# The first layer's modulation in smaller pieces, in front of the products that need it

## The chip, the cores and the metric

One core of one Trainium2 chip. The time is the device time of one execution in microseconds, given as the median of the runs.

## What is computed

A trunk of four layers over a sequence of 256 context rows and 256 rows of x, width 1024, in float32. The layers are a gated spatial unit (layer 0), an RWKV layer, an attention layer, and a gated spatial unit again (layer 3). Each layer first normalises its input and modulates it by a shift and a scale that come from a conditioning vector (one for the context, one for x). The case is about the start of layer 0:

```python
def ada_modulation(cond, w, b):
    m = jax.nn.silu(cond) @ w + b                       # w: 1024 x 3072
    shift, scale, gate = jnp.split(m, 3, axis=-1)
    return shift[..., None, :], scale[..., None, :], gate[..., None, :]

def sgu_mixer(h, w_in, gain, w_s, b_s, w_out):          # w_in: 1024 x 6144
    u, v, z = jnp.split(h @ w_in, 3, axis=-1)
    u = jax.nn.gelu(u)
    v = rms_norm(jax.nn.gelu(v), gain)
    ...
    return (s * jax.nn.silu(z)) @ w_out

# in reference(), layer i:
shift, scale, gate = ada_modulation(c, ada_w[i], ada_b[i])
h = rms_norm(x) * (1 + scale) + shift
x = x + gate * sgu_mixer(h, *sgu_args)                  # and the same for ctx with c_ctx
```

## The kernel before

The 512 rows (context and x) are held transposed as `xT`: eight blocks `k` of 128 features by 512 columns of time. Products are made in a split form: each float32 operand is cast to the narrower type `fp32r` as a high part, and the rest becomes a low part; hi·hi, hi·lo and lo·hi are summed, so that one product of blocks is three matmuls. A weight tile is loaded by `wload` (line 170): a transfer of 1 MB into `raw` (three buffers), a cast of the whole tile into `hi` on ScalarE (ACT, line 183) and a subtraction into `lo` on VectorE (DVE, line 184); `hi` and `lo` have two buffers each. `wparts` with `parts` over 1 does the cast and the subtraction in that many slices, of which all but the first have their subtraction on GpSimd.

**The modulation of layer 0.** Its weights (12 MB) are six chunks of 512 columns: chunks 0 and 1 are the shift, 2 and 3 the scale, 4 and 5 the gate, so that feature block k has its shift in chunk k // 4 and its scale in chunk 2 + k // 4. `ada_load` (line 201) brings a chunk in four transfers of 512 KB into tiles named `adaw`, taken from a ring of 20 buffers that also holds the pairs `hp`. `ada_first` (line 210) multiplies a chunk with the conditioning vectors: eight matmuls `adap` (two instructions each in the trace) in four column groups, a copy `m4` by ACT (line 221), four matmuls `adaT` with a selection matrix (eight instructions) that put the sums across the partitions and so turn them into columns, two additions of the bias on DVE (line 228, context and x), and for the scale one more for "1 +" (line 230). `m4`, the row norm `rstd` and the working tiles `h` share four buffers.

**The norm and the modulated blocks.** `norm_mod` (line 288) makes for each block k: `h = xT * rstd` on DVE (line 292), scale and shift of the context half on ACT (line 297) and of the x half on DVE (line 295), then the split, a cast on ACT (line 304) and a subtraction on DVE (line 305), into the pair `hp`.

**The value products.** In `sgu` (line 349) the columns of v are made in four blocks `c` of 512. For each there are two halves of the weights (`half`, four feature blocks each); each feature block k gives twelve matmuls (four row blocks of 128, three matmuls each, lines 375 to 377). So one half is 48 matmuls, and the whole of v is 384. In the text a "product" of these counts is one such matmul.

**The order around the change.** The program is written down in one sequence. A scheduler orders each engine's instructions when the program is built: of those that its model holds to be ready it takes the first in the written sequence, so that a later product can be put into a gap, and the order is then fixed. Transfers are issued on SyncE's queue (SP), in their order. Before, the sequence is: load chunk 0, the first value weights (transfer and cast), load chunk 2; the row norm; compute chunks 0 and 2, load chunks 1 and 3 (`first`); modulate blocks 0 to 3; the 48 products of half 0; compute chunks 1 and 3 (`early`), modulate blocks 4 to 7; load and cast the second value weights; the 48 products of half 1; then the other column blocks. Chunks 4 and 5 follow later in the layer (`later`). The other three layers' modulation is made on DVE (`ada_rest`, line 232), written behind the layer and put into gaps of it.

## Time and profile before

| | |
|---|---|
| median of 3 runs | 1621.2 us (1619.01 to 1622.14) |
| the profiled execution, its own time | 1616.74 us |
| its span, first to last instruction | 1615.0 us |
| TensorE busy | 1516.5 us (94%) |
| VectorE busy | 1151.3 us (71%) |
| ScalarE busy | 788.0 us (49%) |
| mean granted clock of TensorE | 0.97 |

The profile is of one execution. PE is TensorE's matmuls and PEld its weight loads, DVE is VectorE, ACT ScalarE, POOL GpSimd, SP SyncE. Matmuls are pipelined: a row's duration is longer than the step from one matmul to the next, which is read from their starts. The granted clock is a share of TensorE's full 2.4 GHz; 0.5 is its lower level, 1.2 GHz.

### The profile page before, as it was taken

What the parts mean: (1) busy time and instruction counts of PE and PEld (TensorE: products, weight loads), DVE (VectorE), ACT (ScalarE), POOL (GpSimd) and SP (SyncE); (2) the same over time, 40 slices, a digit from 0 to 9 for tenths busy, and PEclk for the clock granted to TensorE, in tenths of its full rate; (3) what the DMA queues carried; (4) which work ended last, traced back from release to release, by engine and by line L of the source; (5) the groups of instructions that cost most, each with busy time, mean ns of one, the idle gap of its engine ahead of it and who ended that gap; (6) DMA issues with size and microseconds to landing.
All of it is one profiled execution on the core that took longest, in us unless ns stands there. A gap on an engine that the chain in (4) does not pass through costs nothing.

```text
span 1615.0 us, 28890 instructions
## 1 busy us (share of the span) xinstructions
PE 1516.5 (94%) x11666; PEld 1173.8 (73%) x11666; DVE 1151.3 (71%) x2101; ACT 788.0 (49%) x1404; POOL 124.8 (8%) x156
## 2 busy tenths in 40 slices
PE   5999999999599998899899899899999999979998
PEld 2787888888467644777676677678777777768887
DVE  3789998845788367586796854778766666665876
ACT  4544231222455353444445333569866766456543
POOL 0000000000500142212303000000000000000000
PEclk8999999999799999799999999999999999989999
DMA  9676658631044553432433133134321232265452
GB/s 366 242 288 232 234 192 305 233 105 52 36 145 167 174 159 77 145 90 80 126 103 87 59 113 103 62 129 137 121 76 47 78 92 92 66 234 196 169 183 79
DMA packets 95174, 229.05 MB, mean 142 GB/s; under 512 B 26048, under 2 KB 52160, under 8 KB 80576
## 3 DMA queue, kind: packets, MB, share of 16 engines
q1 hardware_dynamic: 92736, 223.00, 41.1%
q10 hardware_dynamic: 2304, 4.20, 0.7%
q8 instruction: 92, 1.51, 0.4%
q14 instruction: 42, 0.34, 0.1%
HBM read 208.81 MB, written 17.83 MB: 140 GB/s over the span
## 4 chain that ended last, share of the span: by engine, by line
PE 46%; DVE 6%; ACT 6%; issue 1%; POOL 1%; DMA 0%; ACTq 0%; DVEq 0%; POOLq 0%
PE fm L310 4%; PE op L310 4%; PE pg L904 3%; PE op L975 2%; PE fm L311 2%; PE op L311 2%; PE pz L310 2%; PE pu L310 2%; PE po L1286 2%; PE sc L1304 2%; PE pe L790 2%; PE sc L1305 1%; PE pv L376 1%; PE pz L311 1%; PE pv L377 1%
## 5 line engine op out<-in xcount | busy, mean ns | idle before, releaser
L184 DVE TENSOR_TENSOR lo<-raw,hi 128x2048 fp32r<-128x2048 f32 (+3 forms) x147 | 247.2, 1683 | 105.0 <-ACT hi L183 104.4
L183 ACT CAST hi<-raw 128x2048 fp32r<-128x2048 f32 (+3 forms) x161 | 212.3, 1324 | 218.8 <-PE op L314 40.5
L251 DVE SCALAR_TENSOR_TENSOR junk<-adaw,scb 128x1024 f32<-128x1024 f32 x112 | 136.9, 1222 | 13.6 <-DMA adaw<-in_ada_wT 11.7
L310 PE MATMUL op<-s,hi 128*128 128x512 f32 x256 | 91.6, 400 | 0.0
L375 PE MATMUL pv<-hi,hp 128*128 128x512 f32 x192 | 76.6, 401 | 9.1 <-ACT hi L183 6.0
L376 PE MATMUL pv<-lo,hp 128*128 128x512 f32 x192 | 76.4, 398 | 1.7 <-DVE lo L184 1.7
L310 PE MATMUL fm<-hx,hi 128*128 128x512 f32 x200 | 73.8, 409 | 4.1 <-ACT hx L304 3.8
L377 PE MATMUL pv<-hi,hp 128*128 128x512 f32 x192 | 76.2, 397 | 0.0
L904 PE MATMUL pg<-xz,wz 128*128 128x256 f32 x256 | 71.1, 412 | 0.0
L311 PE MATMUL op<-s,lo 128*128 128x256 f32 x256 | 71.1, 280 | 0.0
L313 PE MATMUL pj<-xs,hi 128*128 128x512 f32 x128 | 53.9, 423 | 12.3 <-ACT xs L304 10.2
L794 DVE TENSOR_TENSOR E<-pe,masks 128x512 f32<-128x512 f32 x64 | 41.6, 683 | 26.6 <-PE pe L790 23.9
L695 POOL TENSOR_TENSOR BK<-f 64x256 f32<-64x256 f32 x64 | 56.5, 882 | 44.3 <-DVE f L688 31.2
L311 PE MATMUL fm<-hx,lo 128*128 128x256 f32 x200 | 56.5, 287 | 2.0 <-DVE lo L184 2.0
L1004 PE MATMUL pv<-wv,xv 128*128 128x512 f32 x128 | 57.3, 596 | 0.0
L310 PEld LDWEIGHTS op<-s,hi 128*128 128x128 f32 x256 | 48.1, 188 | 12.6 <-issue 1.3
L314 PE MATMUL pj<-xs,hi 128*128 128x512 f32 x128 | 52.7, 412 | 4.0 <-DVE xs L305 4.0
L310 PE MATMUL fm<-cq,hi 128*128 128x512 f32 x144 | 55.7, 423 | 0.0
L904 PEld LDWEIGHTS pg<-xz,wz 128*128 128x128 f32 x256 | 47.1, 197 | 11.5 <-issue 3.6
L975 PE MATMUL op<-Y,wo 128*128 128x256 f32 x192 | 53.8, 415 | 1.3 <-DVE xT L979 1.3
L315 PE MATMUL pj<-xs,lo 128*128 128x512 f32 x128 | 52.5, 412 | 2.2 <-DVE lo L184 2.1
L313 PE MATMUL pu<-hp,hi 128*128 128x512 f32 x128 | 50.7, 396 | 0.0
(392 smaller groups left out, 4027.3 us busy)
## 6 DMA issues: line engine op xcount, KB each, us to landing
adaw<-in_ada_wT SPq DMA_DIRECT2D x36, 1024.0 KB, 6.2
raw<-in_sgu_v SPq DMA_DIRECT2D x16, 1024.0 KB, 5.9
raw<-in_sgu_u SPq DMA_DIRECT2D x16, 1024.0 KB, 5.3
raw<-in_sgu_z SPq DMA_DIRECT2D x16, 1024.0 KB, 5.0
raw<-in_sgu_o SPq DMA_DIRECT2D x16, 1024.0 KB, 4.8
adaw<-in_ada_w SPq DMA_DIRECT2D x24, 512.0 KB, 10.2
xz<-xz SPq DMA_DIRECT2D x32, 256.0 KB, 3.9
raw<-in_ml_z SPq DMA_DIRECT2D x16, 512.0 KB, 3.7
```

What stands on the lines that cost most here:

```text
L183: S.copy(hi[:, sl], raw[:, sl])
L184: (nc.gpsimd if parts > 1 and i else V).tensor_tensor(lo[:, sl], raw[:, sl], hi[:, sl], ALU.subtract)
L251: V.scalar_tensor_tensor(out=junk, in0=raw[:, f, :], scalar=1.0, in1=scb[:, c, :], op0=ALU.mult, op1=ALU.mult, accum_out=m[:, t * 2 + f, c ...
L310: PE.matmul(p, whi, x, start=start, stop=False)
L311: PE.matmul(p[:, 0:256], wlo, x[:, 0], start=False, stop=stop)
L313: PE.matmul(p, whi, x[:, 0], start=start, stop=False)
L375: PE.matmul(pv[tb], hs[k][:, 0, sl], whi[:, ws_], start=k == 0, stop=False)
L376: PE.matmul(pv[tb], hs[k][:, 0, sl], wlo[:, ws_], start=False, stop=False)
L377: PE.matmul(pv[tb], hs[k][:, 1, sl], whi[:, ws_], start=False, stop=k == 7)
L904: PE.matmul(p, ws[k // 4][:, k % 4, pr * 128:pr * 128 + 128], xs[k // 2][:, k % 2, :], start=k == 0, stop=k == 7)
L975: PE.matmul(p[:, ob], w[:, k, ob, :], y[:, k], start=k == 0, stop=k == 1)
L1004: PE.matmul(p, xv[:, k, tb * 128:tb * 128 + 128], ws[k // 4][:, k % 4, :], start=k == 0, stop=k == 7)
```

## The change

The weights of the first modulation are laid out in eight pieces instead of six chunks (`PIECES`): shift and scale for blocks 0 and 1 (256 columns each), the same for blocks 2 and 3, the same for blocks 4 to 7 (512 columns each), and the two halves of the gate as before. A tile `adaw` keeps its size; it holds four feature blocks of 256 columns or two of 512. `ada_first` takes the width from the piece: half as many columns in each matmul, and two instead of four matmuls with the selection matrix, for a piece of 256.

The sequence becomes: load pieces 0 and 1, the transfer of the first value weights, load pieces 2 to 5, the transfer of the second value weights; the row norm; the cast of the first value weights in four parts of 512 columns; pieces 0 and 1, modulate blocks 0 and 1, products of block 0; pieces 2 and 3, modulate blocks 2 and 3, products of blocks 1 and 2; pieces 4 and 5, modulate blocks 4 to 7, products of block 3; the cast of the second value weights in four parts; products of blocks 4 to 7. `wload` is cut in two for this: `wraw` (the transfer) and `wcut` (cast and subtraction, in parts); here all parts of the subtraction are on VectorE.

```diff
--- before.py
+++ after.py
@@ -18,6 +18,8 @@
 T = 512
 RMS_EPS = 1e-6
 
+PIECES = [(c + s, n) for c, n in ((0, 256), (256, 256), (512, 512)) for s in (0, D)] + [(2 * D, 512), (2 * D + 512, 512)]
+
 
 def fm_tiles(w, kb, ob):
     n = w.shape[1] // (ob * 128)
@@ -40,7 +42,8 @@
     f = np.float32
     o["xT"] = np.concatenate([a["ctx"][0], a["x"][0]], 0).T.reshape(KD, 128, T).transpose(1, 0, 2)
     o["cond"] = np.stack([cols(a["c_ctx"]), cols(a["c"][0])], -1)
-    o["ada_w0"] = a["ada_w"][0].reshape(KD, 128, 6, 512).transpose(2, 1, 0, 3).reshape(6, 128, KD * 512)
+    w0 = a["ada_w"][0].reshape(KD, 128, 3 * D)
+    o["ada_w0"] = np.concatenate([w0[:, :, c:c + n].transpose(1, 0, 2).reshape(128, KD * n) for c, n in PIECES], 1)
     o["ada_wT"] = a["ada_w"][1:4].transpose(0, 2, 1).reshape(3, 12, 2, 128, D).transpose(0, 1, 3, 2, 4).reshape(3, 12, 128, 2 * D)
     o["condr"] = np.stack([a["c_ctx"], a["c"][0]])[None]
     o["ada_b"] = np.stack([cols(a["ada_b"][i]) for i in range(4)], 1)
@@ -170,18 +173,29 @@
     def wload(src, n=None):
         return next(wparts(src, n))
 
-    def wparts(src, n=None, parts=1):
-
+    def wraw(src, n=None):
         wp, size = env["w"], env["wn"]
         n = n or size
         raw = wp.tile([128, size], F32, tag="raw", name="raw", bufs=env["raw"])
         nc.sync.dma_start(out=raw[:, :n], in_=src)
+        return raw, n
+
+    def wparts(src, n=None, parts=1):
+
+        yield from wcut(*wraw(src, n), parts, nc.gpsimd)
+
+    def wsplit(raw, parts):
+        *_, w = wcut(*raw, parts)
+        return w
+
+    def wcut(raw, n, parts, other=V):
+        wp, size = env["w"], env["wn"]
         hi = wp.tile([128, size], F32R, tag="hi", name="hi", bufs=env["hi"])
         lo = wp.tile([128, size], F32R, tag="lo", name="lo", bufs=env["hi"])
         for i in range(0, n, n // parts):
             sl = slice(i, i + n // parts)
             S.copy(hi[:, sl], raw[:, sl])
-            (nc.gpsimd if parts > 1 and i else V).tensor_tensor(lo[:, sl], raw[:, sl], hi[:, sl], ALU.subtract)
+            (other if parts > 1 and i else V).tensor_tensor(lo[:, sl], raw[:, sl], hi[:, sl], ALU.subtract)
             if parts > 1:
                 yield hi, lo
         yield hi, lo
@@ -202,31 +216,33 @@
 
         raws = {}
         for n in chunks:
-            for q in range(4):
-                raws[n, q] = env["a"].tile([128, 2, T], F32, tag="p", name="adaw", bufs=env["npair"])
-                nc.sync.dma_start(out=raws[n, q].rearrange("p k c -> p (k c)"), in_=I["ada_w0"][n, :, q * 1024:q * 1024 + 1024])
+            at0, w = sum(w for _, w in PIECES[:n]) * KD, PIECES[n][1]
+            raws[n] = []
+            for q in range(w // 128):
+                t = env["a"].tile([128, 1024 // w, w], F32, tag="p", name="adaw", bufs=env["npair"])
+                nc.sync.dma_start(out=t.rearrange("p k c -> p (k c)"), in_=I["ada_w0"][:, at0 + q * 1024:at0 + q * 1024 + 1024])
+                raws[n] += [t[:, k, :] for k in range(1024 // w)]
         return raws
 
     def ada_first(chunks, raws):
 
         pt = ps("adaT")
         for n in chunks:
+            c0, w = PIECES[n]
             pm = ps("adap")
             for h in range(2):
                 for kk in range(4):
                     k = h * 4 + kk
-                    PE.matmul(pm[32 * kk:32 * kk + 32, :], scp[:, k, :], raws[n, k // 2][:, k % 2, :],
-                              start=(h == 0), stop=(h == 1), tile_position=(0, 32 * kk))
+                    PE.matmul(pm[32 * kk:32 * kk + 32, 0:w], scp[:, k, :], raws[n][k], start=(h == 0), stop=(h == 1), tile_position=(0, 32 * kk))
             m4 = at("m4")
-            S.copy(m4, pm)
+            S.copy(m4[:, 0:w], pm[:, 0:w])
             yield
-            for q in range(4):
-                f = n * 4 + q
-                PE.matmul(pt[:, 2 * f:2 * f + 2], m4[:, q * 128:(q + 1) * 128], sel2, start=True, stop=True)
-            f = slice(n * 4, n * 4 + 4)
+            f = slice(c0 // 128, (c0 + w) // 128)
+            for q in range(w // 128):
+                PE.matmul(pt[:, 2 * (f.start + q):2 * (f.start + q) + 2], m4[:, q * 128:(q + 1) * 128], sel2, start=True, stop=True)
             for c in range(2):
                 V.tensor_tensor(mods[0][:, f, c], pt[:, 0:48].rearrange("p (f c) -> p f c", c=2)[:, f, c], ada_b[:, 0, f], ALU.add)
-            if n in (2, 3):
+            if D <= c0 < 2 * D:
                 V.tensor_scalar(mods[0][:, f, :], mods[0][:, f, :], 1.0, None, ALU.add)
 
     def ada_rest():
@@ -346,16 +362,15 @@
             yield
 
 
-    def sgu(j, m, t0, done=None, first=None, early=None, later=(), head=None):
+    def sgu(j, m, t0, done=None, early=None, later=(), head=None):
         later = iter(later)
         n = T - t0
         tbs = list(range(t0 // 128, 4))
         r = norm_rstd(t0)
         head = head or wload(I[f"sgu_v{j}"][0])
-        if first:
-            first()
         hs = [pair("hp") for _ in range(KD)]
-        norm_mod(m, t0, hs, r, range(4 if early else 8))
+        if not early:
+            norm_mod(m, t0, hs, r, range(8))
         ss = const.tile([128, 4, 4], F32, tag="ss", name="ss")
         v = {}
         for c in range(4):
@@ -363,12 +378,15 @@
                 next(later, None)
             pv = {tb: ps("pv") for tb in tbs}
             for half in range(2):
-                if early and (c, half) == (0, 1):
-                    early()
-                    norm_mod(m, t0, hs, r, range(4, 8))
-                whi, wlo = wload(I[f"sgu_v{j}"][c * 2 + half]) if c + half else head
+                if early and c == 0:
+                    whi, wlo = wsplit(next(head), 4)
+                else:
+                    whi, wlo = wload(I[f"sgu_v{j}"][c * 2 + half]) if c + half else head
                 for kk in range(4):
                     k = half * 4 + kk
+                    if early and c == 0:
+                        for kn in early(k):
+                            norm_mod(m, t0, hs, r, [kn])
                     for tb in tbs:
                         sl = slice(tb * 128, tb * 128 + 128)
                         ws_ = slice(kk * 512, kk * 512 + 512)
@@ -1360,24 +1378,28 @@
         for k in range(KD):
             sq_add(k, 0)
         act_set("natural_log_exp_and_others")
-        raws = ada_load((0,))
-        head0 = wload(I["sgu_v0"][0])
-        raws.update(ada_load((2,)))
-
-        def first():
-            interleave(ada_first((0, 2), raws))
-            raws.update(ada_load((1, 3)))
+        raws = ada_load((0, 1))
+        head0 = [wraw(I["sgu_v0"][0])]
+        raws.update(ada_load((2, 3, 4, 5)))
+        head0.append(wraw(I["sgu_v0"][1]))
+
+        def early(k):
+
+            n, ks = {0: ((0, 1), (0, 1)), 1: ((2, 3), (2, 3)), 3: ((4, 5), (4, 5, 6, 7))}.get(k, ((), ()))
+            if n:
+                interleave(ada_first(n, raws))
+            return ks
 
         def later():
-            r4 = ada_load((4,))
+            r4 = ada_load((6,))
             yield
-            yield from ada_first((4,), r4)
-            r5 = ada_load((5,))
+            yield from ada_first((6,), r4)
+            r5 = ada_load((7,))
             yield
             yield
-            yield from ada_first((5,), r5)
-
-        sgu(0, mods[0], 0, first=first, early=lambda: interleave(ada_first((1, 3), raws)), later=later(), head=head0)
+            yield from ada_first((7,), r5)
+
+        sgu(0, mods[0], 0, early=early, later=later(), head=iter(head0))
         for _ in ada_rest():
             pass
     rwkv(mods[1])
```

## Rows read from the trace of the kernel before

**Rows 1.** The page's table of engines: busy time, its share of the span, and the number of instructions.

```profile
PE 1516.5 (94%) x11666; PEld 1173.8 (73%) x11666; DVE 1151.3 (71%) x2101; ACT 788.0 (49%) x1404; POOL 124.8 (8%) x156
```

**Rows 2.** Busy time by stretches of the span. Columns: the stretch and its length in us; then, engine by engine, busy us and (instructions); the mean granted clock of TensorE as a share of full speed; the mean busy share of the 16 DMA engines; GB/s.

```profile
11.90:30.40 18.50, 13.52 (x50) 3.83 (x50) 5.70 (x12) 6.65 (x11) 0.00 (x0) 0.84 1.02 408
30.40:43.40 13.00, 12.97 (x48) 10.39 (x48) 5.90 (x7) 4.15 (x5) 0.00 (x0) 0.83 0.84 328
49.10:410.00 360.90, 359.27 (x1676) 296.75 (x1672) 285.19 (x425) 121.09 (x153) 0.36 (x8) 1.00 0.56 204
```

**Rows 3.** The timeline of all engines from 13 to 31 us, the rows of the chain to the first product. Columns: start, duration, engine, line, operation, output<-inputs, shape, count, and in brackets the idle time before it with what ended it. Rows of one kind that follow each other are merged: a duration is then that of the whole group, waits inside it included.

```profile
13.88 4.46 PE L218 MATMUL adap<-adaw,scp 128*32 128x512 f32 x16
...
14.77 0.63 ACT L279 ACTIVATE rstd<-rstd 128x512 f32<-128x512 f32 x1
...
16.80 0.19 PEld L218 LDWEIGHTS adap<-adaw,scp 128*32 128x32 f32 x4 [1.02 <-DMA adaw<-in_ada_w]
18.39 0.59 ACT L221 COPY m<-adap 128x512 f32<-128x512 f32 x1 [2.99 <-PE adap L218]
19.03 1.05 PE L225 MATMUL adaT<-sel,m 128*128 128x2 f32 x8 [0.69 <-ACT m L221]
19.28 1.90 ACT L183 CAST hi<-raw 128x2048 fp32r<-128x2048 f32 x1 [0.31 <-DMA raw<-in_sgu_v]
20.12 0.23 DVE L228 TENSOR_TENSOR mod<-adaT,ada_b 128x4 f32<-128x4 f32 x2 [8.36 <-PE adaT L225]
...
24.42 0.19 PEld L218 LDWEIGHTS adap<-adaw,scp 128*32 128x32 f32 x4 [1.09 <-DMA adaw<-in_ada_w]
...
28.09 0.17 DVE L230 TENSOR_SCALAR mod<-mod 128x8 f32<-128x8 f32 x1
28.29 1.58 ACT L297 ACTIVATE h<-h,mod 128x256 f32<-128x256 f32 x3 [2.09 <-DVE mod L230]
```

**Rows 4.** The issues on SyncE's queue (SPq) from the same timeline (start, and time from the first issue of the group to the end of its last), and the cast of the second half of the value weights, which waited for the first of the last four transfers to land.

```profile
7.22 2.46 SPq L207 DMA_DIRECT2D adaw<-in_ada_w  x4
10.06 0.33 SPq L178 DMA_DIRECT2D raw<-in_sgu_v  x1
10.43 14.29 SPq L207 DMA_DIRECT2D adaw<-in_ada_w  x12
...
25.66 16.04 SPq L178 DMA_DIRECT2D raw<-in_sgu_v  x4
...
37.11 1.91 ACT L183 CAST hi<-raw 128x2048 fp32r<-128x2048 f32 x1 [2.85 <-DMA raw<-in_sgu_v]
```

**Rows 5.** The timeline of TensorE alone, from the first product to where it stops waiting. Between the first two rows shown stand nine more products, between the second and the third 37.

```profile
30.43 0.79 PE L375 MATMUL pv<-hi,hp 128*128 128x512 f32 x1 [3.12 <-ACT hp L304]
...
34.87 0.42 PE L376 MATMUL pv<-lo,hp 128*128 128x512 f32 x1
...
43.64 1.92 PE L218 MATMUL adap<-adaw,scp 128*32 128x512 f32 x16
46.29 1.05 PE L225 MATMUL adaT<-sel,m 128*128 128x2 f32 x8 [0.73 <-ACT m L221]
47.28 1.92 PE L218 MATMUL adap<-adaw,scp 128*32 128x512 f32 x16
49.13 0.50 PE L375 MATMUL pv<-hi,hp 128*128 128x512 f32 x1
...
50.17 0.95 PE L225 MATMUL adaT<-sel,m 128*128 128x2 f32 x8
50.98 0.47 PE L376 MATMUL pv<-lo,hp 128*128 128x512 f32 x1
```

**Rows 6.** Groups of instructions in the first 62 us by line and shape: count | busy us, mean ns of one | idle time before them with what ended it.

```profile
L184 DVE TENSOR_TENSOR lo<-raw,hi 128x2048 fp32r<-128x2048 f32 x3 | 6.9, 2293 | 9.3 <-ACT hi L183 9.3
L305 DVE TENSOR_TENSOR hp<-h,hp 128x512 fp32r<-128x512 f32 x8 | 5.3, 690 | 2.9 <-ACT hp L304 2.9
L304 ACT CAST hp<-h 128x512 fp32r<-128x512 f32 x8 | 4.6, 614 | 0.4 <-DVE h L295 0.4
L297 ACT ACTIVATE h<-h,mod 128x256 f32<-128x256 f32 x8 | 4.5, 596 | 6.3 <-DVE mod L230 4.4 <-DVE h L292 1.9
L295 DVE TENSOR_SCALAR h<-h,mod 128x256 f32<-128x256 f32 x8 | 2.9, 408 | 0.1
```

**Rows 7.** The instructions of line 1112, a copy of 256 columns from PSUM in the last but one layer: minimum, median and maximum duration in ns, and the first and last start.

```profile
L1112 ACT COPY z<-fm x16: 349/354/376, 1091.8 to 1152.4; 128x256 f32<-128x256 f32 x16
```

**Rows 8.** Busy time by stretches again (columns as in rows 2), cut where the granted clock changes.

```profile
21.00:25.00 4.00, 4.00 (x16) 0.57 (x12) 3.50 (x3) 0.18 (x1) 0.00 (x0) 0.57 1.03 409
25.00:28.00 3.00, 1.62 (x12) 0.97 (x8) 0.65 (x3) 0.59 (x1) 0.00 (x0) 1.00 1.02 412
28.00:30.40 2.40, 0.00 (x0) 0.00 (x0) 1.32 (x5) 2.11 (x5) 0.00 (x0) 0.51 1.01 410
30.40:35.00 4.60, 4.57 (x11) 3.56 (x12) 3.60 (x6) 2.24 (x4) 0.00 (x0) 0.51 1.03 419
```

**Rows 9.** One more stretch (columns as in rows 2), and the instructions of line 251, the products of the other layers' modulation (durations in ns, first and last start).

```profile
160.00:200.00 40.00, 40.00 (x187) 33.41 (x186) 39.04 (x58) 10.78 (x12) 0.00 (x0) 1.00 0.63 222
L251 DVE SCALAR_TENSOR_TENSOR junk<-adaw,scb x112: 1211/1224/1227, 64.2 to 325.0; 128x1024 f32<-128x1024 f32 x112
```

## Prediction

> **What bounds the kernel now.** I read the page first. TensorE (PE) is busy for 1516.5 of 1615.0 us, VectorE (DVE) for 1151.3 [rows 1], so time can only be won where PE stands idle or is slow. The busy time by stretches shows where that is [rows 2]. Between 49.1 and 410 us PE has 359.27 of 360.90 us, and a list of its waits over that stretch is empty. So a microsecond won ahead of 49.1 us is kept at least to 410 us, unless something else becomes late. Ahead of 49.1 us PE has 13.52 of 18.50 us while the transfers run at full load (DMA share 1.02), and then 12.97 of 13.00 us at a mean granted clock of 0.83.
>
> The timeline of the start gives the chain [rows 3]. The first modulation group (2 MB) has its last tile at 16.80 us, the value weights are there at 19.28, the second group's last tile is there at 24.42. Its shift and scale are on DVE until 28.26; only then are the first blocks modulated, and the first product starts at 30.43. The issue rows, with the landing of the second weights [rows 4], show the order in the one SP queue behind this: first group, weights, second group, the other two groups; twelve issues spread over 14.29 us, so the queue runs at the pace of the transfers. On PE [rows 5], ten products run from 30.43 to 34.87 (0.44 us each) and 38 from there to 43.64 (0.231 each). Then come the other two groups, 43.64 to 49.13, with a wait of 0.73 us for a copy, and their last transposes at 50.17 (0.81 us until the next product). From 49.13 on PE runs products of the next block of columns while it waits, so nothing stands idle.
>
> **The ledger of before.** I count PE's time from its first product until the first 48 products and the shift and scale groups are done: 13.2 us of products (30.43 to 43.64), 5.5 us for the two later groups (43.64 to 49.13), 0.8 us of transposes. Sum 19.5, from 30.43: 49.9 us. The changed kernel is to be compared at this point; behind it both do the same work.
>
> **The change, part by part.** *The first product, earlier.* Two pieces of 256 columns (shift and scale of blocks 0 and 1) make the same 2 MB as the first group and stand at its place in the queue, so their last tile lands at 16.80 too. From there to the copy was 1.59 us for 512 columns; for 256 I allow half of that to all of it (0.8 to 1.6). The copy costs 0.35 us for 256 columns [rows 7] to 0.59 for 512 [rows 3]; the transposes half of 1.05; two adds and the plus one 0.23 + 0.17. With 0.1 for hand-overs: 19.0 to 19.9 us. Then ScalarE (ACT) has to modulate (0.60) and cast (0.61) block 0 [rows 6], but the cast of the value weights now stands in four parts ahead of it in program order, ready at 19.28. The trace has no such part; the nearest row is the cast of 128x512, 0.61, so 2.5 us for four against 1.90 for the whole. If all four go first, the first product starts at 19.28 + 2.5 + 0.60 + 0.61 = 23.0; if only one does, at about 21.2; with a second modulation between, 23.5. I take 23.0, the order of the program.
>
> *Work that moves behind the first product.* The pieces of blocks 2 and 3 (landed by 24.42, the second group's time) were hidden ahead of the first product and are now on PE in the middle of the products: 1.92 us of matmuls, if 256 columns cost half of 512, and 0.97 of transposes: 2.9 us. At full price a piece would cost 1.92, so 4.8 is the upper bound. The two later pieces of 512 columns keep their 1.92 + 0.97 + 1.85 + 0.81 = 5.6 us; the wait of 0.73 goes, since products stand ready beside it (if each of the four pieces waits, it is 2.9 more). The 48 products keep their 13.2 us, ten at the low level of the clock. Sum: 13.2 + 2.9 + 5.6 = 21.7 us, from 23.0: 44.7.
>
> *Are the data there?* Products of block 0 end at 27.9, so the second pair (24.42) is waited for by nobody. It takes PE to 30.8, block 1 takes it to 33.6; block 2 is modulated by about 30.8 + 0.4 + 0.60 + 0.61 = 32.4. The last pair is 4.2 MB behind 24.42; at 408 GB/s [rows 2] it lands at 34.7, and PE comes to it at 36.4, behind block 2. Its modulation ends at 42.0, block 4 is ready at 43.6, and block 3 keeps PE until 44.7. The second value weights land where they did, 37.11 [rows 4]. So every wait is covered, but by about 1 us only.
>
> *Costed at nothing.* Weight parts on DVE: four of 0.69 [rows 6] for one of 2.29, 0.5 us more per load, twice; block 0 needs the first part alone, and each later block finds PE with 2.8 us of products against 0.69 + 0.69 + 0.41 of DVE work. Without that cover it is the 1.0 us itself. The copy and two adds for each of two more pieces lie under products in the same way (0.35 + 0.23 each). The number of transfers and of bytes is unchanged; the second weights' transfer stays behind the twelve tiles on SP, so no later load is pushed back. In SBUF the last four block pairs wait for tiles of the first two pieces, which are free by 18.4.
>
> *The clock.* The granted clock was 0.57 from 21 to 25, 1.00 from 25 to 28, and 0.51 from 28 to 35, ten products into the stream [rows 8]. The fall at 28 came with an idle PE; the rise at 25 came after matmuls that waited for tile upon tile. Bounds: the ten slow products at the high level, 10 x (0.444 - 0.231) = 2.1 us less; another ten at the low one, 2.1 more. I keep ten. Against this change speaks a rule of the Trainium skill ("TensorE: Matmul & The Clock Gate", section "HAM oscillation — how this bites in real kernels"): a loop that puts a short group of matmuls between waits for its next transfer comes back to the half clock at each group. By it the 21.7 us would become 38.3, the second rival below; the rows agree with it in part only, since the stretch that waited for tile upon tile ended at the high level (1.00 from 25 to 28).
>
> **The sum.** 49.9 - 44.7 = 5.2 us. Bounds added up: 1.8 (first product) and 2.1 (clock) more, 9.1; or 0.5, 1.9, 2.9 and 2.1 less, -2.2. They don't fall together, so the forecast's own range is a gain of 2.5 to 8. The profiled execution takes 1616.74 us by its own time, so it would take 1611.5; it is 4.5 below the median of the runs (1621.2), from which the forecast is 1616.0 us, its own range 1613 to 1619. The three runs lie 3.1 us apart; a change under 0.2% (3.2 us) can't be told from none here.
>
> **Rivals.** *All pieces ahead of the products.* Each engine's order is fixed when the program is built. If the plan reckons the transfers to land sooner than they do, PE has all six pieces in front of the first product. The last lands at 34.7; 1.9 us of matmuls, 1.3 of copy, transposes and adds, 1.2 for block 0: first product at about 39, 13.2 us on: 52, but nothing left to do then. As block 1 could still be covered by fewer pieces, I put it at 47 to 52, about 49.4: a gain of 0.5, 1620.7 us. For it: DVE stood idle 8.36 us before the first adds [rows 3], with the row norm ready from 15.40 on, which the next multiplications wait for; so the order isn't free. Against it: at 49.13 the plan had put four products between a copy and its transposes, so it knows such gaps.
>
> *Slow clock throughout (slower).* The 21.7 us of work at the low level: products 48 x 0.444 = 21.3 instead of 13.2, the pieces 17.0 instead of 8.5; 16.6 more, 1632.6 us. It decides from where the low level lasts 10.4 us longer than the 4.4 of before (each such microsecond costs a half): there the gain is gone, and 6.4 us on it is slower by the 3.2. For it: PE's work comes in pieces between waits. This is the case that the section of the Trainium skill named above ("TensorE: Matmul & The Clock Gate") describes. Against it: by the times above PE has something to do all along from 23.0.
>
> *The gain is given back later.* From 160 to 200 us DVE is busy 39.04 of 40 us [rows 9]; if it is the real limit there, PE can't run 5 us earlier and waits for a split of weights; the gain ends between 0 and 2, 1620.2 us. Against it: much of that is the other layers' modulation, 112 products of 1.22 us from 64.2 to 325.0 [rows 9], which nobody needs before PE's full stretch ends at about 410 [rows 2]; it can give way.
>
> *Better.* First product at 21.2 and no slow products: a gain of 9, 1612.2.
>
> **How the numbers follow.** Forecast 0.62, better 0.08, all pieces ahead 0.12, given back 0.11, slow clock 0.07. Faster by over 0.2%: better and nearly all of the forecast, 0.68. Within: a rest of the forecast, all ahead, given back, 0.25. Slower: the slow clock, 0.07. The range 1611 to 1621 holds the forecast with the runs' scatter, most of "better" and about half of the two cases of little gain, some 0.8.
>
> **What would show it.** Right: first product (value weights times block 0) near 23, three pairs of pieces on PE with products between them, 48 products and the pieces done near 44.7, PE full from there, and all later marks, as the end of PE's full stretch at about 410, 5 us earlier. Wrong: three pairs in a row ahead of the products; a granted clock near 0.5 beyond 30; PE waiting for a DVE split between 100 and 330; or a first product later than 24 because ACT has something else first.

## The result, and the profile after

The changed kernel takes 1629.25 us (median of 8 runs, 1622.88 to 1634.8); the kernel before, in the runs made beside it, takes 1618.58. The ratio is 1.0070, 95% interval 1.0054 to 1.0086: slower by 0.7%, where 1616.0 and a gain of 0.3% had been forecast. The profiled execution of after takes 1634.64 us, with a span of 1632.9.

The page's row of engines, which answers to [rows 1], shows TensorE busy for 10.9 us more in a span that is 17.9 longer:

```profile
PE 1527.4 (94%) x11698; PEld 1182.2 (72%) x11698; DVE 1152.2 (71%) x2112; ACT 788.7 (48%) x1412; POOL 125.4 (8%) x156
```

Busy time by stretches (columns as in [rows 2], the first four stretches the same, then three cut where the clock changes; each fence of windows below has the order PE, PEld, DVE, ACT, POOL, clock, DMA share, GB/s):

```profile
11.90:30.40 18.50, 12.47 (x70) 6.62 (x70) 6.34 (x16) 6.71 (x13) 0.00 (x0) 0.72 1.01 404
30.40:43.40 13.00, 6.92 (x42) 4.67 (x38) 4.79 (x14) 4.49 (x10) 0.00 (x0) 0.72 0.90 366
49.10:410.00 360.90, 358.91 (x1677) 294.07 (x1676) 286.14 (x423) 121.82 (x153) 0.00 (x0) 1.00 0.56 204
...
33.00:36.00 3.00, 0.60 (x3) 0.16 (x1) 0.00 (x0) 0.00 (x0) 0.00 (x0) 1.00 1.04 429
39.70:43.40 3.70, 3.70 (x12) 2.66 (x12) 3.22 (x10) 2.12 (x5) 0.00 (x0) 0.50 0.59 230
60.00:66.00 6.00, 6.00 (x20) 4.42 (x19) 5.19 (x12) 5.97 (x8) 0.00 (x0) 0.72 0.56 193
```

The loss is in the second row: from 30.4 to 43.4 us TensorE works for 6.92 of 13 us, where it worked for 12.97 before [rows 2]. Its timeline shows the place. This is the stretch of [rows 5]; where rows are left out, only products stand:

```profile
23.85 0.79 PE L393 MATMUL pv<-hi,hp 128*128 128x512 f32 x1 [4.71 <-ACT hp L320]
...
29.40 1.07 PE L236 MATMUL adap<-adaw,scp 128*32 128x256 f32 x16
...
31.63 1.07 PE L236 MATMUL adap<-adaw,scp 128*32 128x256 f32 x16
...
39.68 1.01 PE L242 MATMUL adaT<-sel,m 128*128 128x2 f32 x4 [6.08 <-ACT m L238]
40.55 0.77 PE L393 MATMUL pv<-hi,hp 128*128 128x512 f32 x1
...
43.39 3.35 PE L236 MATMUL adap<-adaw,scp 128*32 128x512 f32 x10
46.66 0.50 PE L393 MATMUL pv<-hi,hp 128*128 128x512 f32 x1
...
49.62 1.06 PE L236 MATMUL adap<-adaw,scp 128*32 128x512 f32 x6
...
52.53 1.92 PE L236 MATMUL adap<-adaw,scp 128*32 128x512 f32 x16
...
57.00 0.40 PE L395 MATMUL pv<-hi,hp 128*128 128x512 f32 x1
59.39 2.30 PE L393 MATMUL pv<-hi,hp 128*128 128x512 f32 x5 [1.99 <-ACT hi L197]
```

The first product comes at 23.85, 6.6 us earlier than before. Twelve products of block 0, the third piece, three products of block 1, its transposes, the fourth piece, three more products; then PE stands still for 6.08 us, waiting for the copy of the fourth piece by ScalarE (`m`, line 238). Six products of block 1 whose data are there stand behind the transposes in PE's order and do not pass. ScalarE's timeline over the same time says why the copy is late:

```profile
21.12 2.16 ACT L197 CAST hi<-raw 128x512 fp32r<-128x512 f32 x4
23.19 1.13 ACT L320 CAST hp<-h 128x512 fp32r<-128x512 f32 x2
30.54 0.37 ACT L238 COPY m<-adap 128x256 f32<-128x256 f32 x1 [6.22 <-PE adap L236]
37.70 1.66 ACT L197 CAST hi<-raw 128x512 fp32r<-128x512 f32 x3 [6.79 <-DMA raw<-in_sgu_v]
39.27 0.36 ACT L238 COPY m<-adap 128x256 f32<-128x256 f32 x1
39.53 0.62 ACT L197 CAST hi<-raw 128x512 fp32r<-128x512 f32 x1
```

Between the copies of the third and the fourth piece stand three of the four casts of the second value weights. They wait 6.79 us for their transfer, until 37.70, and the copy, whose input is there at 32.7 (the end of the fourth piece on PE), waits with them. The cast needs nothing that is late but the transfer; the copy needs nothing that is late at all. Only the order, fixed when the program is built, ties them together. SyncE's issues, the rows that answer to [rows 4]:

```profile
10.36 0.33 SPq L180 DMA_DIRECT2D raw<-in_sgu_v  x1
10.73 13.71 SPq L223 DMA_DIRECT2D adaw<-in_ada_w  x12
25.38 2.96 SPq L180 DMA_DIRECT2D raw<-in_sgu_v  x3
```

The transfers go out as before; the second weights land 0.6 us later than the 37.11 of [rows 4].

**The ledger of after**, from 23.85 to 59.39, where the first 48 products and all pieces are done and the next begins: 35.5 us, against the 21.7 of the sum. Of the 13.8 us between them, two waits are 8.1 (6.08 and 1.99). After the long wait the granted clock is 0.50: six products 0.43 us apart instead of 0.23 (1.2 us), ten matmul instructions of a piece 3.27 us instead of the 1.84 of a later run (1.4), transposes 0.87 instead of 0.44 (0.4); 3.0 in sum. The first slow stretch holds twelve products, not ten: 0.4. The fifth piece is cut into ten and six instructions and takes a third round, 1.0 (told at the end). The remaining 1.3 I put down to PE's change-overs between products and pieces, some 0.1 each (30.40 to 30.74: 0.34 from the product behind a piece to the next, where 0.23 is the step). Against the 49.9 of before that is 9.5 us late, and the 1.99 of idle time is followed by another slow stretch (0.72 from 60 to 66), some 1.7 us more (nine steps of 0.42 us instead of 0.23, 59.39 to 63.20).

**Carried to the end.** PE is full again from there (358.91 of 360.90 us), so the loss stays. The first matmul of the spatial mixing (`pm`) marks the end of the stage; the two rows are of before and of after, in two fences, with durations in ns and the first and last start:

```profile
L420 PE MATMUL pm<-ws,v x192: 270/275/356, 154.1 to 1588.2; 128*128 128x128 f32 x192
```

```profile
L438 PE MATMUL pm<-ws,v x192: 270/275/356, 165.2 to 1606.0; 128*128 128x128 f32 x192
```

11.1 us late at this mark, and 10.7 between the medians. That the two profiled executions lie 17.9 apart has another cause, told behind the experiments.

### The profile page after: what moved, and what is told of

It is laid out like the page before. It is cut to its first block, busy times and chain, and to the rows that moved or that the text cites. A ratio compares the mean times of both kernels' runs of the same rounds, so it can differ in the third digit from the quotient of the medians.

```text
span 1632.9 us, 28976 instructions
## 1 busy us (share of the span) xinstructions
PE 1527.4 (94%) x11698; PEld 1182.2 (72%) x11698; DVE 1152.2 (71%) x2112; ACT 788.7 (48%) x1412; POOL 125.4 (8%) x156
## 4 chain that ended last, share of the span: by engine, by line
PE 78%; DVE 12%; ACT 5%; DMA 3%; issue 1%; POOL 1%; SPq 0%; ACTq 0%; DVEq 0%; POOLq 0%
PE fm L326 5%; PE op L326 4%; PE pv L393 3%; PE pv L394 3%; PE pv L395 3%; PE pg L922 3%; PE fm L327 2%; PE op L993 2%; PE pe L808 2%; PE op L327 2%; PE pu L326 2%; PE pz L326 2%; PE pu L329 2%; PE po L1304 2%; PE pz L329 2%; PE op L329 2%
## 5 line engine op out<-in xcount | busy, mean ns | idle before, releaser
L198 DVE TENSOR_TENSOR lo<-raw,hi 128x2048 fp32r<-128x2048 f32 (+4 forms) x153 | 247.6, 1622 | 106.1 <-ACT hi L197 105.0
L197 ACT CAST hi<-raw 128x2048 fp32r<-128x2048 f32 (+4 forms) x167 | 212.9, 1284 | 224.2 <-PE op L330 40.5
L329 PE MATMUL pj<-xs,hi 128*128 128x512 f32 x128 | 53.0, 415 | 12.6 <-ACT xs L320 10.2
L393 PEld LDWEIGHTS pv<-hi,hp 128*128 128x128 f32 x192 | 37.8, 198 | 25.1 <-ACT hi L197 9.2
```

The source lines that it names most:

```text
L197: S.copy(hi[:, sl], raw[:, sl])
L198: (other if parts > 1 and i else V).tensor_tensor(lo[:, sl], raw[:, sl], hi[:, sl], ALU.subtract)
L329: PE.matmul(p, whi, x[:, 0], start=start, stop=False)
L393: PE.matmul(pv[tb], hs[k][:, 0, sl], whi[:, ws_], start=k == 0, stop=False)
```

## The experiments

All were compared with the kernel before in runs on the same chip. "Mark" is the first start of `pm` in the profiled execution. "Next" is the start of the first product that follows the first 48 (in before: the point 49.9 of the ledger). It is a product of block 4; only in after, both times, and in "casts behind block 3" and "second weights sooner" is it one of block 0 with the weights of the next column block. The median of before was 1617.73 us beside the four kernels from "casts behind block 3", 1618.09 beside the next three, 1616.57 beside the two behind them and 1619.0 beside the last two, so the rows compare by their ratios.

| run | first product | next | mark | median us | ratio to before, 95% |
|---|---|---|---|---|---|
| before | 30.43 | 49.9 | 154.1 | | 1 |
| after | 23.85 | 59.39 | 165.2 | 1629.25 | 1.0070 (1.0054 to 1.0086) |
| after, once more | 24.16 | 59.98 | 165.7 | 1632.14 (one) | |
| casts behind block 3 | 23.69 | 49.65 | 155.1 | 1619.95 | 1.0022 (1.0008 to 1.0036) |
| second weights sooner | 30.06 | 56.32 | 162.0 | 1624.71 | 1.0052 (1.0032 to 1.0072) |
| parts alone | 30.54 | | 154.2 | 1617.22 | 1.0005 (0.9992 to 1.0018) |
| pieces alone | 24.03 | 56.99 | 161.1 | 1626.53 | 1.0065 (1.0042 to 1.0087) |
| last pair sooner | 24.00 | 49.63 | 153.7 | 1620.46 | 1.0015 (0.9999 to 1.0031) |
| first part first | 24.28 | 49.51 | 153.6 | 1618.59 | 1.0008 (0.9992 to 1.0024) |
| warm | 22.56 | 50.52 | 154.6 | 1618.39 | 1.0007 (0.9992 to 1.0022) |
| third pair ahead | 22.40 | 46.59 | 152.1 | 1615.68 | 0.9998 (0.9988 to 1.0009) |
| the same, warm | 24.29 | 46.54 | 152.1 | 1617.66 | 1.0005 (0.9991 to 1.0019) |
| gain scaled later | 22.74 | 45.32 | 151.2 | 1617.66 | 0.9986 (0.9969 to 1.0002) |
| third pair interleaved | 24.56 | 45.98 | 150.0 | 1613.95 | 0.9983 (0.9966 to 1.0000) |

### The casts of the second weights, kept behind block 3

```diff
                 if early and c == 0:
-                    whi, wlo = wsplit(next(head), 4)
+                    with ExitStack() as after:
+                        for i in state["hp", 3] if half else ():
+                            after.enter_context(tc.issue_after(i.ins))
+                        whi, wlo = wsplit(next(head), 4)
```

`state["hp", 3]` are block 3's cast and subtraction; `issue_after` keeps the instructions written under it behind a given one in that engine's order. The data, and the transfers of the pieces and of these weights, stay as they are. PE's order stays too, but for some products of block 2 among themselves; some small loads behind the weights are issued sooner.

> The changed kernel with one thing added: ScalarE's casts and VectorE's subtractions of the second value weights are kept, in the fixed order, behind the split of block 3; TensorE's order stays the same. Theory A (in the changed kernel three of these casts stand in ScalarE's queue in front of the copy of the fourth modulation piece and hold it until their transfer lands at 37.7 us; TensorE waits 6.1 us for it with products standing behind the wait, and falls to the low clock): the copy comes at about 33 us, the 6.1 us wait is gone, the 48 products are done near 48 instead of 57.4, and the median falls by 6 to 10 us, to 1619 to 1623, about the kernel before. Theory B (the small groups between products are themselves what costs, by the low clock and the added matmuls): another wait or a longer stretch at the low clock takes the place of the 6.1 us; the gain is under 3 us, 1626 or more.

ScalarE's timeline:

```profile
32.48 0.37 ACT L238 COPY m<-adap 128x256 f32<-128x256 f32 x1 [1.86 <-PE adap L236]
...
38.09 2.18 ACT L197 CAST hi<-raw 128x512 fp32r<-128x512 f32 x4 [1.75 <-DMA raw<-in_sgu_v]
```

and PE's:

```profile
47.26 0.40 PE L398 MATMUL pv<-hi,hp 128*128 128x512 f32 x1
49.65 2.50 PE L396 MATMUL pv<-hi,hp 128*128 128x512 f32 x5 [1.99 <-ACT hi L197]
```

The copy comes 6.8 us earlier, the wait of 6.08 and the low level of the clock after it are gone, and 10.1 of the 11.1 us at the mark come back. So the order is the cause of the loss. The edit moves VectorE's subtractions of these weights too, and no run tells the two engines apart; it is ScalarE's copy that PE's wait of 6.08 names. But nothing is left of the forecast gain of 5.2: the first product is 6.7 us earlier and the next one behind the 48 only 0.25. From 23.69 the work takes 24.0 us to the end of the 48 products instead of 21.7; and then PE waits 1.99 us. ScalarE casts the next column block's weights, whose `hi` is one of two buffers and is free only when the 48th product has read it. In the kernel before, the same cast ran at the same point, told by ScalarE's timeline there:

```profile
43.74 1.90 ACT L183 CAST hi<-raw 128x2048 fp32r<-128x2048 f32 x1 [4.72 <-PE pv L377]
```

It started when the 48 products were done, and lay under the two later groups' matmuls, which stood *behind* those products [rows 5]. The 5.5 us of matmuls that the change moved ahead of the last products had been the cover of this cast.

### The second weights' transfer sooner

```diff
-        raws.update(ada_load((2, 3, 4, 5)))
+        raws.update(ada_load((2, 3)))
         head0.append(wraw(I["sgu_v0"][1]))
+        raws.update(ada_load((4, 5)))
```

> The changed kernel with the transfer of the second value weights issued in front of the third pair of pieces instead of behind it, so that it lands near 27 us; the third pair lands 2.5 us later, near 37. Theory A: the casts are no longer in the way, since their data are there before the copy is due; the same 6.1 us wait goes as with the order changed, and the median falls to 1619 to 1623. Theory B: no more than 3 us are won, 1626 or more. If the third pair's later landing is what counts, TensorE waits for it near 37 us and up to 2.5 us of the gain are lost.

ScalarE's timeline, and PE's in a second fence:

```profile
27.31 2.18 ACT L197 CAST hi<-raw 128x512 fp32r<-128x512 f32 x4 [1.33 <-DMA raw<-in_sgu_v]
29.39 1.13 ACT L320 CAST hp<-h 128x512 fp32r<-128x512 f32 x2
```

```profile
30.06 0.80 PE L393 MATMUL pv<-hi,hp 128*128 128x512 f32 x1 [8.21 <-ACT hp L320]
...
56.32 2.40 PE L393 MATMUL pv<-hi,hp 128*128 128x512 f32 x5 [1.99 <-ACT hi L197]
```

The weights land 10 us sooner, the fourth piece's copy no longer waits, and the kernel is still slower than before. The plan, which seems to reckon with an earlier landing, now puts these casts in front of the casts of blocks 0 and 1, and the first product waits for them. The late transfer is not the cause by itself: the cast takes the place that the plan gives it, and whatever stands behind it waits.

### Each part alone

Parts alone: chunks of 512 columns as before, the cast in four parts. Pieces alone: the pieces, but each weight tile cast as a whole.

```diff
# parts alone
-PIECES = [(c + s, n) for c, n in ((0, 256), (256, 256), (512, 512)) for s in (0, D)] + ...
+PIECES = [(c + s, 512) for c in (0, 512) for s in (0, D)] + ...
# pieces alone
-                if early and c == 0:
-                    whi, wlo = wsplit(next(head), 4)
-                else:
+                if True:
                     whi, wlo = wload(I[f"sgu_v{j}"][c * 2 + half]) if c + half else head
```

> The casts in parts alone: the modulation in the six chunks of 512 of the kernel before, computed where it was (two chunks ahead of the first product, two behind the first 48), with the transfers of both value weights issued early and their casts in four parts as in the changed kernel. Theory A: no copy that TensorE's next products need stands behind the casts here, because the second weights are wanted only after all 48 products; the median is that of the kernel before within 3 us, 1616 to 1621. If the parts are what costs, it is slower than before by 5 us or more.

> The pieces alone: pieces of 256 and 512 computed where the changed kernel has them, but both value weights cast whole by one instruction at the places where the kernel before writes it. The second weights' cast stands again in front of the fourth piece's copy in ScalarE's fixed order. Theory A: the same wait, some 6 us near 33 to 39 us plus 1 for the longer cast, and a time near the changed kernel, 1626 to 1632. If the cast in parts were the cause, the time would be that of the kernel before, 1616 to 1621.

Parts alone is the kernel before (1.0005, mark 154.2). Pieces alone has most of the loss, by the same rows on ScalarE and then on PE:

```profile
37.28 1.90 ACT L197 CAST hi<-raw 128x2048 fp32r<-128x2048 f32 x1 [5.25 <-DMA raw<-in_sgu_v]
39.09 0.36 ACT L238 COPY m<-adap 128x256 f32<-128x256 f32 x1
```

```profile
39.51 0.61 PE L242 MATMUL adaT<-sel,m 128*128 128x2 f32 x4 [4.55 <-ACT m L238]
```

So the cut of the cast costs nothing that can be told from none, and is not what holds the copy; the pieces between the products, which put two copies of ScalarE into the time in which the weights are on their way, are.

### Three steps towards the forecast: last pair sooner, first part first, warm

From here each kernel has the one above it and one more edit. *Last pair sooner*: block 3's products kept behind the third pair's matmuls, so that the pair's chain is covered by them. *First part first*: only the first part of the first weights' cast stands in front of the casts of blocks 0 and 1. *Warm*: two matmuls whose result nobody reads, between the second piece's transposes and the first product.

```diff
+                    if early and (c, k) == (0, 3):
+                        after.enter_context(tc.issue_after(state["adap", 5].ins))
...
-                        whi, wlo = wsplit(next(head), 4)
+                        rest = wcut(*next(head), 4)
+                        whi, wlo = next(rest)
...
+                        if k == 0:
+                            with tc.issue_after(state["hp", 1][0].ins), tc.issue_after(state["hp", 1][1].ins):
+                                list(rest)
...
+                                for _ in range(2):
+                                    PE.matmul(pw, ones, xT[:, 0, :], start=True, stop=True)
```

> The kernel of the first experiment (casts of the second value weights behind block 3), and in TensorE's fixed order the products of block 3 stand behind the matmuls of the third pair of pieces. In the first experiment the third pair's transposes ended at 46.5 us, the 48 products at 47.7, and then TensorE waited 2.0 us (for the cast of the next column block's weights, whose buffer is free only after the 48th product) and ran slow for some 4 us. Theory C (what is left of the loss is that the 48 products no longer have the third pair's matmuls behind them to cover that cast and the modulation of block 4): with block 3's products as cover the wait falls from 2.0 to 0.5 us or less, the slow stretch behind it goes, and the median is 3 to 4 us below the first experiment's 1619.95, 1616 to 1617. Theory D (the buffers alone set it): the wait of 2 us stays, 1619 to 1621.

> The kernel before this one in the list, and only the first of the four parts of the first value weights is cast ahead of blocks 0 and 1; the other three stand behind the split of block 1. Expected from the sum of the prediction: the first product moves from 23.7 to about 22 us. Theory E (TensorE's own work sets the pace from the first product on): the median falls by the same 1.5 us, to about 1615. Theory F (the third pair's transfer, landed at about 35 us, sets the pace): the earlier start is given back as a wait there, no difference from the kernel before it.

> The kernel before this one in the list with two more matmuls of 512 float32 columns that nothing uses, in the gap of TensorE between the second piece's transposes and the first product. In the runs so far TensorE stood idle there from 18.9 us and then ran its first 12 products at the low clock, 0.45 us each instead of 0.23. Theory G (the slow clock at the first products is the rest of the loss): they run at the high clock, 2.5 us less, and the median falls by up to 2.5 us against the kernel without them. If the pace is set elsewhere behind them, or the two matmuls don't hold the clock up, no difference.

Last pair sooner cuts the wait behind the 48 products from 1.99 to 0.75 us and the slow products after it disappear; the next product starts at the same time, and no gain can be told in the medians. First part first is no better in the table, and does not tell theories E and F apart: in this execution the second piece took 1.93 us where it takes 1.07 in the next kernel, both transposes 1.01 instead of 0.61, and the first product came at 24.28 (22.40 in a later kernel with the same edit). Warm did what it was for: its first block runs at 0.23 us a product, and the third pair's matmuls start at 31.85, 3.0 us ahead of the run without it; 1.3 of these are the warming's (33.11 in the later kernel, where the first product comes at 22.40), the rest is that execution's slow start. There it was given back, as ScalarE's rows show, and PE's behind them:

```profile
37.09 2.18 ACT L197 CAST hi<-raw 128x512 fp32r<-128x512 f32 x4 [3.98 <-DMA raw<-in_sgu_v]
39.18 0.57 ACT L238 COPY m<-adap 128x512 f32<-128x512 f32 x1
```

```profile
39.81 1.57 PE L242 MATMUL adaT<-sel,m 128*128 128x2 f32 x8 [2.13 <-ACT m L238]
```

The second weights' casts, behind block 3 in the order, are in front of the *fifth* piece's copy. PE came sooner and waited; a granted clock of 0.50 to 0.58 from 40 to 47 us followed. It is the wait of after, one pair on.

### The third pair ahead of blocks 2 and 3

On *first part first*: the third pair is made ahead of block 2's products, and the second weights' casts stand behind its copies (ScalarE) and its "plus one" (VectorE).

```diff
-                        for i in state["hp", 3] if half else ():
+                        for i in (state["m4", 5], state["one", 5]) if half else ():
...
-                    if early and (c, k) == (0, 3):
+                    if early and (c, k) in ((0, 2), (0, 3)):
...
-            n, ks = {0: ((0, 1), (0, 1)), 1: ((2, 3), (2, 3)), 3: ((4, 5), (4, 5, 6, 7))}.get(k, ((), ()))
+            n, ks = {0: ((0, 1), (0, 1)), 1: ((2, 3), (2, 3)), 2: ((4, 5), (4, 5, 6, 7))}.get(k, ((), ()))
```

> The kernel with the first part first, and two further moves in the fixed orders: the products of blocks 2 and 3 stand behind the matmuls of the third pair of pieces (so that the pair's matmuls run when its transfer has landed, near 35 us, not at 35 and 42), and the casts of the second value weights stand behind the copies of that pair. In the three kernels before it the first product of block 4 or of the next column block came at 49.5 to 50.5 us whatever was won earlier. Theory H (what sets that point is when the third pair's sums are ready, and they came late because the fixed order put products between its matmuls): block 4 is ready near 43, the 48 products and all pieces are done near 45.5 to 46.5, TensorE doesn't wait there, and the median is 3 to 4 us below the kernel before the change, about 1614 to 1615. If it is something else (buffers, the second weights' landing), the point stays at 49 to 50 and the time at 1618.

> The same with the two unused matmuls ahead of the first product that held the high clock there. With them alone, 3.1 us were won by 36.6 us and lost again as a wait of 2.1 us on the third pair's copy, which stood behind the casts that waited for their transfer, and a stretch at the low clock. Theory A, as before: with the casts behind the copies the gain stays, the point near 45.5 comes at 43 to 44, the median is at 1612 to 1613. If the transfer of the third pair sets the pace from 35 us on, there is no difference from the kernel without them.

The mark is now 2.0 us ahead of before (0.4 and 0.5 in *last pair sooner* and *first part first*), but the medians show no difference (ratio 0.9998). The 48 products are done at 45.2. Block 4 starts at 46.59 with 1.35 us of waiting, for its cast on ScalarE, which had waited for the third pair's scale and shift from VectorE. VectorE's timeline, and the issue on SyncE's queue of what it waited for:

```profile
42.65 0.17 DVE L422 TENSOR_SCALAR gh<-sgu_gain 128x16 f32<-128x16 f32 x1 [5.56 <-DMA sgu_gain<-in_sgu_gain]
...
43.94 0.23 DVE L244 TENSOR_TENSOR mod<-adaT,ada_b 128x4 f32<-128x4 f32 x2
```

```profile
25.20 2.96 SPq L180 DMA_DIRECT2D raw<-in_sgu_v  x3
29.05 0.33 SPq L157 DMA_DIRECT2D sgu_gain<-in_sgu_gain  x1
```

A scaling of 0.17 us, of a vector of 8 KB that the layer first uses at 153.3, stands in front of the third pair's additions and waits 5.56 us; its load was issued at 29.05 behind three weight tiles of 1 MB each and was there 13.6 us after that. The same mechanism a third time, on another engine, with another instruction. It was there before this kernel: with the casts behind block 3, this scaling waited 2.02 us and the next one, of the bias vector, 2.17, in front of the third pair's additions and of block 4's and 5's norm. The variant with two warming matmuls waits there too (block 4 at 46.54) and gains nothing: its second piece took 1.93 us and its transposes 1.01 again, its warming matmuls 3.3, and the first product came at 24.29.

### The scaling behind block 7, and the third pair interleaved

```diff
+        with tc.issue_after(state["hp", 7][1].ins):
+            V.tensor_scalar(gh, gain, 0.5, None, ALU.mult)
+            V.tensor_scalar(bh, bs, 0.5, None, ALU.mult)
```

and in the second kernel also, the first two lines ahead of the second layer's constants (`bdm`, `half`, `hvec`, `kab`) and the third behind them,

```diff
+        behind = tc.issue_after(state["hp", 7][1].ins)
+        behind.__enter__()
...
+        behind.__exit__(None, None, None)
...
-                interleave(ada_first(n, raws))
+                interleave(*[ada_first((i,), raws) for i in n]) if n[0] == 4 else interleave(ada_first(n, raws))
```

> The kernel of the run before last (third pair's matmuls ahead of the products of blocks 2 and 3), with the two small scalings of the gain and of the bias vector on VectorE kept behind the split of block 7. Theory (an instruction that waits for a late transfer holds up, in the engine's fixed order, work that has its data): VectorE no longer waits 5.6 us for the small load ahead of the third pair's additions, block 4 is ready before the 48 products end at about 45.2, its first product starts at 45.2 to 45.8, and the time is 3 to 4 us below the kernel before, about 1612.5 to 1614 where that takes 1616.5. Rival 1: the next instruction in VectorE's order waits in its place (the constants of the second layer, or a subtraction of the second value weights), block 4 still starts at 46.5, and the time is 1615.7. Rival 2: the start is won, but the gain does not reach the end (scatter of the clock in the second layer's scan, or a later wait): block 4 at 45.5 and a time within 0.1% of before.

> As the run beside it, and also the constants of the second layer behind the split of block 7, and the third pair's two pieces with both groups of matmuls ahead of both groups of transposes, so that TensorE does not wait for the first copy. Theory: the wait for that copy (up to 0.7 us) goes, the 48 products end at about 44.5, block 4 follows without a wait, and the time is 0.5 to 1 us below the run beside it, about 1612 to 1613. Rival: the second copy comes after the casts of the second value weights in ScalarE's order and the wait returns at another place (block 4 at 46.5 or later, 1616 or more).

In the first, block 4 follows the 48 products at 45.32 without a wait, as expected. Its median is 1.3 us below before (2.3 by the ratio, whose interval reaches no change), not the 3 to 4 expected. The first rival did not come true, but the "later wait" of the second did. The timelines of ScalarE, VectorE and PE:

```profile
48.40 1.92 ACT L255 ACTIVATE t<-scb 128x2048 f32<-128x2048 f32 x1 [2.63 <-DMA scb<-in_condr]
50.23 0.60 ACT L320 CAST hp<-h 128x512 fp32r<-128x512 f32 x1
```

```profile
50.35 2.29 DVE L256 SCALAR_TENSOR_TENSOR t<-t,scb 128x2048 f32<-128x2048 f32 x1 [0.68 <-ACT t L255]
52.56 0.69 DVE L321 TENSOR_TENSOR hp<-h,hp 128x512 fp32r<-128x512 f32 x1
```

```profile
53.30 0.50 PE L407 MATMUL pv<-hi,hp 128*128 128x512 f32 x1 [1.45 <-DVE hp L321]
```

Block 6 is modulated by 44.5 us. Its cast on ScalarE stands behind an instruction of the other layers' modulation (`t`, line 255), which waits 2.63 us for the load of its vector `scb`; its subtraction on VectorE stands behind 2.29 us of work on the same `t`, and PE waits 1.45 for it. The constant `bdm` of the second layer waits for its load as well, 1.83 us, but is done at 49.3, before block 6 is cast, and holds nothing up here. In the second kernel block 6's cast comes at 45.32, ahead of `t`; which of its edits moved it no run tells. There the list of PE's waits from 12 to 420 us ends with the first product and two short waits for copies, and the stretches show PE full from there:

```profile
PE ssq L299 <- DVE acc L288: 15.1, 2, 12.6
PE pj L329 <- ACT xs L320: 10.2, 1, 10.2
PE pv L405 <- ACT hp L320: 3.1, 1, 3.1
PE adaT L242 <- ACT m L238: 1.0, 2, 0.5
```

```profile
30.40:43.40 13.00, 13.00 (x97) 8.49 (x96) 6.91 (x22) 6.54 (x14) 0.00 (x0) 1.00 1.02 413
...
48.00:54.00 6.00, 6.00 (x28) 4.96 (x27) 5.23 (x4) 5.58 (x6) 0.00 (x0) 1.00 0.83 306
```

(The wait of 10.2 for `xs` is the second layer's first projection at 419 us.) From the first product to block 4 it takes 45.98 - 24.56 = 21.4 us, close to the 21.7 of the prediction's sum, in part by luck: some eight slow products instead of ten make up for change-overs that the sum left out. Its mark is 4.1 us ahead of before's. The median is 1613.95, beside 1619.0 of before in the same session; the interval of the ratio, 0.9966 to 1.0000, just reaches no change. It beats the changed kernel clearly (all but one of its 12 runs lie under 1618.1, all 8 of after's over 1622.8); that it beats the kernel before is likely, not shown.

### The changed kernel once more, and the scatter

> The changed kernel once more, for a second trace. Its first one was 17.9 us longer than that of the kernel before, of which 11.1 stand by the end of the value products and 6.7 more come up in the scan of layer 1 (574 to 920 us). Theory A: the first part is there again, 10 to 12 us, with the wait of 6 us on the copy; the second part is scatter of the clock in the scan and will be another, between 0 and 7 us.

The repeated profile has the same wait (6.46 us at 40.43) and the same mark (165.7), so the loss is there again. The first product does vary: the second piece's matmuls take 1.07 us in eight of the twelve profiled executions that have pieces and 1.93 in four (second weights sooner, first part first, third pair ahead warm, third pair interleaved), and the kernels with the first part first then have their first product at 24.3 to 24.6 instead of 22.4 to 22.7. Why is open. What varies more is the second layer: the matmuls `pn` of line 717 in before (`nab` in the trace, the chunks' inverses of the RWKV layer) span 331.0 to 341.4 us from first to last start in the 14 profiled executions, 334.1 in before and 341.4 in the first profile of after. The other stretches, from the mark to these matmuls (409 to 412), from them to the third layer's scores (251.7 to 254.1) and from there to the end of the execution by its own time (464.2 to 465.2), are steady within 3 us. From 574 to 920 us the mean granted clock is 0.95 in before, 0.92 in after and 0.96 in the last kernel; but the last kernel's matmuls span 338.2, more than before's, so the clock alone does not account for it, and the cause is open. So 11.1 us between the two profiles of before and after are the change, and 7 are this scatter, which stands in every comparison above; a start that is 4 us better is at the edge of what 12 runs tell.

## Why the prediction was wrong

*First product: right, by errors that nearly cancel.* 23.85 against 23.0. The cast of the first weights did go ahead of blocks 0 and 1 in four parts, 2.16 us against the 2.5 reckoned. But it began at 21.12 and not at 19.28 with the weights' landing: ScalarE first waited for the pieces' sums until 20.12 and modulated both blocks.

*Pieces on PE: right in price, not in manner.* A piece of 256 costs 1.00 us, its transposes 0.44: 2.9 for the pair, as in the sum. The three pairs came with products between them, so the rival "all pieces ahead" was not what happened. What the sum lacked was the cut piece (1.0) and the change-overs (1.3).

*"The second value weights land where they did, 37.11 ... So every wait is covered": the step that failed.* The landing was right within 0.6 us. I asked of each transfer only when the products that need it come, and not what stands behind the cast that waits for it in ScalarE's order; "Costed at nothing" has the copies of the two more pieces under products, at 0.35 us. Before, the cast that waited until 37.11 [rows 4] had nothing behind it that anyone needed before 43.6; after, the fourth piece's copy stood there, and PE waited 6.08 us for it, with 3.0 more by the low level of the clock behind it. The written sequence puts the second weights' cast after block 3's products and so seems to speak against it, but the plan may draw an instruction forward where its model holds the data to be there, as the prediction itself says in "all pieces ahead". I used this against PE's order alone.

*"Behind it both do the same work": failed too, by 2.0 us and a slow stretch.* The sum compared where PE's work ends and took the next product to be ready. The next column block's cast can start only at the 48th product's end, since `hi` has two buffers; before, 5.5 us of pieces lay over it [rows 5]. With the first fault repaired, 0.7 at the first product, 2.3 of PE's own work behind it (the cut piece, the change-overs, two more slow products) and this 2.0 took nearly all of the 5.2.

*The clock: the condition of the rival "slow clock throughout" was met, as a consequence.* It decided from 10.4 us of low level beyond the 4.4 of before. After shows about 5.2 (23.85 to 29), 7.0 (39.7 to 46.7) and 3.4 (60.0 to 63.4), 15.6 in sum, 11.2 beyond the 4.4. The last two follow the two waits; with the waits gone the low level is gone from there (0.50 at 39.7 to 43.4 in after, 1.00 from 30 to 48 where the casts stand behind block 3). It added 3.0 and 1.7 us to the 8.1 of the two waits, and was not their cause. That this rival's 1632.6 lies nearer to the result than the forecast is luck, for its sum has no wait in it.

*"Given back later": not by the mechanism named.* The last kernel's 4.1 us at the mark show no wait for a split up to 410. But two of the steps towards the forecast, *warm* and the scaling behind block 7, gave gain back within 20 us, behind the next instruction that waited for a transfer.

*Bounds.* The range allowed 2.9 for waits that are met by each piece, but no wait of the length of a transfer. Its upper end, 1621, was too low by 8.

## What to carry to other kernels

Where a transfer lands late, look at the engine that consumes it: what stands behind the waiting instruction in its order, and who needs that? Earlier work needs this asked again of every transfer in flight, small constants included, since what was in front of the late one before may now be behind it, and what covered a cast or a load may have moved ahead of it. An instruction that waits for data which only a later stage needs belongs, in the order, behind the last instruction of the stage that runs meanwhile.

## What the runs showed of the hardware that I had not expected

A group of 512 columns in four column groups (16 instructions) takes 1.85 us; when the order cut it in ten and six instructions with products between, the ten took 1.84 (35.06 to 36.90 us in the kernel with the casts behind block 3) and the six 0.99. With the pieces alone a piece was cut at two: 0.97 for the two and 1.85 for the fourteen. The times fit rounds of eight instructions, some 0.93 us each: either cut makes three rounds of two.

The granted clock of a stretch and the pace of its products can differ: in the last kernel the column shows 1.00 for 21 to 25 and 25 to 28 us, while the first products there, 24.56 to 27.71, stand 0.43 us apart, the pace at 0.50 elsewhere. The steps from start to start are the surer reading.

Two waits with different aftermaths: after 1.99 us without work behind the 48 products (casts behind block 3) the next products came 0.43 apart until 52.4 (clock 0.72 from 48 to 54); after 0.75 at the same place (last pair sooner), 0.23 apart at once (1.00), as after 1.45 at 53.30 with the gain scaled later.
